# SiLU times gate: loads and stores moved to GpSimd's one queue, each transfer as a single packet

## The chip, the cores and the metric

The kernel runs on one core of one Trainium2 chip. A core has five engines with their own instruction streams: TensorE (not used here), VectorE (DVE in the profile), ScalarE (ACT), GpSimd (POOL) and SyncE (SP). Data moves between the chip's main memory (HBM) and the core's working memory (SBUF, 128 partitions) by 16 DMA engines. A transfer is issued from the queue of one of the engines; every issuer's transfers run on the same 16 DMA engines. The metric is device time in microseconds (us), the median of several runs.

## The reference

The input `x` is fp32 of shape 32 x 512 x 2048. The last dimension is cut in two halves, and the output, 32 x 512 x 1024, is SiLU of the first half times the second:

```
x1, x2 = x[..., :1024], x[..., 1024:]
silu_x1 = x1 * (1 / (1 + np.exp(-x1)))
out = silu_x1 * x2
```

That is 134.22 MB read and 67.11 MB written, with one SiLU and one multiplication per output element.

## The kernel before

The input is taken as 16,384 rows of 2048 numbers and cut into 16 tiles of 1,024 rows. In a tile each of the 128 partitions holds K = 8 rows that follow each other in HBM, so a partition's part of a load is one run of 65,536 B and its part of a store one run of 32,768 B. A load moves 8 MiB, a store 4 MiB.

There are two input buffers (`xt`) and two output buffers (`ot`), from two pools with `bufs=2`. Nothing is reordered by a scheduler (`manual_schedule`): each engine runs its instructions in the order of the program, and semaphores make an instruction wait for what it needs.

For tile i the kernel runs `silu` (line 86, ScalarE, from `xt` into `ot`), then `mul` (line 93, VectorE, in place in `ot`), then stores `ot` (line 112, issued on ScalarE's queue), then issues the load of tile i + 2 into the input buffer that has just come free (line 82, SyncE's queue). Loads 0 and 1 are issued ahead of the loop; load 0 is moved ahead of the program's first barrier by `issue_ahead_of_the_first_barrier`, which takes the first load that it finds, on whichever engine.

Two tiles are cut finer. Tile 0 is computed in four pieces of two rows per partition (KC_EDGE = 2), and its store is issued in five pieces, named in `OPENING` by partitions and rows: the first needs only the first piece of two rows. Tile 15 is computed in two halves (KS = 4), each stored by itself (line 120).

Loads and stores stand in two queues of their own, SyncE's and ScalarE's. A load has to wait until the multiplication of the tile that used its buffer is done, and a SiLU until the store that used its output buffer is done.

Of the kernel before, what the change touches and what calls it, by code (L numbers as in the profile page):

```python
# [1 line left out]

# [4 lines left out]


def issue_ahead_of_the_first_barrier(nc):

    head, body = nc.main_func.blocks[:2]
    load = next(ins for ins in body.instructions if type(ins).__name__ == "InstDMACopy")
    at = next(
        j for j, ins in enumerate(head.instructions)
        if ins.engine == load.engine and type(ins).__name__ == "InstDrain"
    )
    body.instructions = [ins for ins in body.instructions if ins.name != load.name]  # L20
    head.instructions = head.instructions[:at] + [load] + head.instructions[at:]


@with_exitstack
def kernel(
    ctx: ExitStack,
    tc: tile.TileContext,
    x: bass.AP,
    out: bass.AP,
):  # L30

    nc = tc.nc
    P = nc.NUM_PARTITIONS

    x_flat = x.flatten_outer_dims()  # L40
    out_flat = out.flatten_outer_dims()
    num_rows, in_cols = x_flat.shape
    half = in_cols // 2
    dt = x_flat.dtype

    K = 8
    KC_EDGE = 2
    KS = 4
    OPENING = [
        (slice(0, None, 4), slice(0, 2)),  # L50
        (slice(2, None, 4), slice(0, 4)),
        (slice(2, None, 4), slice(4, None)),
        (slice(0, None, 4), slice(2, None)),
        (slice(1, None, 2), slice(None)),
    ]
    PLAN = [K] * (num_rows // (P * K))

    in_pool = ctx.enter_context(tc.tile_pool(name="in_pool", bufs=2))
    out_pool = ctx.enter_context(tc.tile_pool(name="out_pool", bufs=2))

    plan = []
    row = 0
    for k in PLAN:
        plan.append((row, k))
        row += P * k
    assert row == num_rows
    n_tiles = len(plan)

    def view(flat, i):
        row0, k = plan[i]  # L70
        return flat[row0:row0 + P * k].rearrange("(p k) d -> p k d", k=k)

    nc.at_finalize(issue_ahead_of_the_first_barrier)


    ctx.enter_context(tc.manual_schedule())

    loaded = {}

    def load(i):  # L80
        xt = in_pool.tile([P, K, in_cols], dt, name="xt")
        nc.sync.dma_start(out=xt[:, :plan[i][1], :], in_=view(x_flat, i))
        loaded[i] = xt

    def silu(ot, xt, c, ce):
        nc.scalar.activation(  # L86
            out=ot[:, c:ce, :],
            in_=xt[:, c:ce, :half],
            func=mybir.ActivationFunctionType.Silu,
        )  # L90

    def mul(ot, xt, c, ce):
        nc.vector.tensor_mul(  # L93
            out=ot[:, c:ce, :],
            in0=ot[:, c:ce, :],
            in1=xt[:, c:ce, half:],
        )

    load(0)
    load(1)  # L100
    for i in range(n_tiles):
        xt = loaded.pop(i)
        ov = view(out_flat, i)
        ot = out_pool.tile([P, K, half], dt, name="ot")
        if i < n_tiles - 1:
            kc = KC_EDGE if i == 0 else K
            for c in range(0, K, kc):
                silu(ot, xt, c, c + kc)
                mul(ot, xt, c, c + kc)

            for ps, ks in OPENING if i == 0 else [(slice(None), slice(None))]:
                nc.scalar.dma_start(out=ov[ps, ks], in_=ot[ps, ks])
            if i + 2 < n_tiles:
                load(i + 2)
            continue
        for c in range(0, K, KS):
            silu(ot, xt, c, c + KS)
            mul(ot, xt, c, c + KS)
        for c in range(0, K, KS):
            nc.scalar.dma_start(out=ov[:, c:c + KS], in_=ot[:, c:c + KS])  # L120


# [1 line left out]
_INS = ['x']  # L124
_OUTS = [((32, 512, 1024), 'float32')]


# [23 lines left out]
```

## Time and profile before

| What | Value |
|---|---|
| Time, median of 3 runs | 470.35 us (470.28 to 472.34) |
| Span of the profiled execution | 468.4 us |
| DMA: loads (queue q1) | 134.22 MB, 2304 packets, 66.4% of the 16 engines' span |
| DMA: stores (queue q10) | 67.11 MB, 2576 packets, 33.2% |
| Mean rate over the span | 430 GB/s |
| VectorE busy | 139.3 us (30%), 14 full multiplications of 8.69 us |
| ScalarE busy | 114.1 us (24%), 14 full SiLUs of 7.03 us |
| GpSimd busy | 0.2 us |
| Load, median from issue to landing | 35.1 us |
| Full store, median from issue to landing | 42.2 us |

The profile is of one execution. Its span goes from the first to the last instruction on the core; a time on the device has some launch and end around it, and the median of the runs is 1.95 us above this span. The profiled execution's time from launch to end is not given apart from the span.

In the slices each digit is the busy share of one fortieth of the span, in tenths. In the DMA row it is the mean over the 16 engines. The share of a queue is the time that its packets took out of 16 engines times the span. The chain is the work that ended last, followed back from the last instruction; each of its lines has a start, a length and what ran. In the timeline a line has a start, a length, the engine (with a q for its queue), the line of the program, the instruction and how many of them, and in brackets the idle time ahead of it and what ended it. The trace also holds a record of each DMA packet: queue, start, length and size.

### The profile page before, as it was taken

What the parts mean: (1) busy time and instruction counts of PE and PEld (TensorE: products, weight loads), DVE (VectorE), ACT (ScalarE), POOL (GpSimd) and SP (SyncE); (2) the same over time, 40 slices, a digit from 0 to 9 for tenths busy, and PEclk for the clock granted to TensorE, in tenths of its full rate; (3) what the DMA queues carried; (4) which work ended last, traced back from release to release, by engine and by line L of the source; (5) the groups of instructions that cost most, each with busy time, mean ns of one, the idle gap of its engine ahead of it and who ended that gap; (6) DMA issues with size and microseconds to landing.
All of it is one profiled execution on the core that took longest, in us unless ns stands there. A gap on an engine that the chain in (4) does not pass through costs nothing.

```text
span 468.4 us, 185 instructions
## 1 busy us (share of the span) xinstructions
DVE 139.3 (30%) x20; ACT 114.1 (24%) x21; POOL 0.2 (0%) x4
## 2 busy tenths in 40 slices
DVE  0070600704207042070520605116061150602543
ACT  1142305005050050601406014060230602306060
POOL 0000000000000000000000000000000000000000
DMA  9899999999999999999999999899999899999998
GB/s 442 364 470 425 448 403 403 493 403 403 448 465 431 403 442 409 493 403 414 437 448 448 403 448 465 386 448 439 411 493 442 372 439 493 403 448 403 428 423 358
DMA packets 4880, 201.33 MB, mean 430 GB/s; under 512 B 592, under 2 KB 592, under 8 KB 592
## 3 DMA queue, kind: packets, MB, share of 16 engines
q1 hardware_dynamic: 2304, 134.22, 66.4%
q10 hardware_dynamic: 2576, 67.11, 33.2%
HBM read 134.22 MB, written 67.11 MB: 430 GB/s over the span
## 4 chain that ended last, share of the span: by engine, by line
DMA 72%; DVE 14%; ACT 11%; DVEq 1%; issue 0%
DMA out_dram<-ot 63%; DVE ot L93 14%; ACT ot L86 11%; DMA xt<-in_x_dram 9%; DVEq L146 1%
## 5 line engine op out<-in xcount | busy, mean ns | idle before, releaser
L93 DVE TENSOR_TENSOR ot<-ot,xt 128x8192 f32<-128x8192 f32 (+2 forms) x20 | 139.3, 6983 | 321.1 <-ACT ot L86 321.1
L86 ACT ACTIVATE ot<-xt 128x8192 f32<-128x8192 f32 (+2 forms) x20 | 112.8, 5661 | 340.2 <-DMA out_dram<-ot 305.8
L86 ACT ACT_TABLE_LOAD x1 | 1.3, 1283 | 0.8 <-PEq L135 0.8
L135 POOL MEMSET const-bfloat16-1.0<- 128x1 bf16 x1 | 0.1, 102 | 0.0
L135 POOL MEMSET const-uint8-127<- 128x1 uint8 x1 | 0.1, 102 | 0.0
L135 POOL MEMSET const-float32-1.0<- 128x1 f32 x1 | 0.1, 99 | 0.0
L135 POOL MEMSET const-float32-0.0<- 128x1 f32 x1 | 0.1, 98 | 0.2 <-issue 0.2
## 6 DMA issues: line engine op xcount, KB each, us to landing
out_dram<-ot ACTq DMA_DIRECT2D x14, 4096.0 KB, 42.2
out_dram<-ot ACTq DMA_DIRECT2D x3, 2048.0 KB, 6.9
out_dram<-ot ACTq DMA_DIRECT2D x2, 512.0 KB, 17.6
out_dram<-ot ACTq DMA_DIRECT2D x1, 768.0 KB, 28.2
xt<-in_x_dram SPq DMA_DIRECT2D x16, 35.1
out_dram<-ot ACTq DMA_DIRECT2D x1, 256.0 KB, 11.3
```

Source lines behind the costliest of these rows:

```text
L86: nc.scalar.activation(out=ot[:, c:ce, :], in_=xt[:, c:ce, :half], func=mybir.ActivationFunctionType.Silu,)
L93: nc.vector.tensor_mul(out=ot[:, c:ce, :], in0=ot[:, c:ce, :], in1=xt[:, c:ce, half:],)
L135: nc = _bacc.Bacc("TRN2", target_bir_lowering=False, num_devices=1)
L146: with _tile.TileContext(nc) as tc:
```

## The change

Loads 0 and 1 stay on SyncE's queue and the last tile's two stores on ScalarE's. All others, stores 0 to 14 and loads 2 to 15, are issued from GpSimd's queue, in the order store 0, load 2, store 1, load 3 and so on, each with `single_packet=True`: on each DMA engine, a transfer's descriptors make up one packet. Tile 0 is still computed in four pieces, but stored as one transfer, and `OPENING` is gone. Nothing else in the computation changes.

```
@@ tile_split_silu_mul_kernel @@
-    OPENING = [
-        (slice(0, None, 4), slice(0, 2)),
-        (slice(2, None, 4), slice(0, 4)),
-        (slice(2, None, 4), slice(4, None)),
-        (slice(0, None, 4), slice(2, None)),
-        (slice(1, None, 2), slice(None)),
-    ]
@@ load(i) @@
         xt = in_pool.tile([P, K, in_cols], dt, name="xt")
-        nc.sync.dma_start(out=xt[:, :plan[i][1], :], in_=view(x_flat, i))
+        if i < 2:
+            nc.sync.dma_start(out=xt, in_=view(x_flat, i))
+        else:
+            nc.gpsimd.dma_start(out=xt, in_=view(x_flat, i), single_packet=True)
         loaded[i] = xt
@@ the loop over tiles @@
-            for ps, ks in OPENING if i == 0 else [(slice(None), slice(None))]:
-                nc.scalar.dma_start(out=ov[ps, ks], in_=ot[ps, ks])
+            nc.gpsimd.dma_start(out=ov, in_=ot, single_packet=True)
             if i + 2 < n_tiles:
                 load(i + 2)
```

## The prediction

> **What bounds the kernel now.** I read the time slices first, then the DMA queues, the chain of waits, the groups by form, and last the trace's packet records.
>
> ```profile
> span 468.4 us, 185 instructions
> ...
> DVE  0070600704207042070520605116061150602543
> ACT  1142305005050050601406014060230602306060
> ...
> DMA  9899999999999999999999999899999899999998
> ...
> DMA packets 4880, 201.33 MB, mean 430 GB/s; under 512 B 592, under 2 KB 592, under 8 KB 592
> ...
> q1 hardware_dynamic: 2304, 134.22, 66.4%
> q10 hardware_dynamic: 2576, 67.11, 33.2%
> ```
>
> The DMA row is at 9 nearly everywhere while VectorE and ScalarE are mostly idle. The two queues together fill 66.4 + 33.2 = 99.6% of the 16 engines' span. So the kernel is bound by the DMA engines, and a change can win only what is in the missing 0.4% (1.9 us) and in overhead inside packets. It can lose whatever leaves the engines without work.
>
> The chain, in order of time, shows the opening and the steady period:
>
> ```profile
> 0.78 42.99 DMA xt<-in_x_dram
> ...
> 43.79 7.04 ACT ot L86
> ...
> 50.85 8.70 DVE ot L93
> ...
> 59.58 45.22 DMA out_dram<-ot
> ...
> 104.82 7.04 ACT ot L86
> ...
> 111.88 8.70 DVE ot L93
> ...
> 120.60 42.19 DMA out_dram<-ot
> ...
> 162.82 7.04 ACT ot L86
> ```
>
> Load 1 has landed by 43.77. In the steady part two tiles take 162.82 - 104.82 = 58.00 us, so one takes 29.00. Computing a tile takes 7.04 + 8.70 and three steps of 0.02, that is 15.8. The reader should see that 15.8 is far below 29.00: arithmetic matters only if the engines run out of queued transfers while it goes on.
>
> The packet records say what those 29.00 us are. A load is 8 packets of 65,536 B on each engine, 2.418 us each (19.34), and a full store 8 of 32,768 B, 1.213 us each (9.70); together 29.04. A packet of 16,384 B takes 0.611, so doubling it to 32,768 adds 0.602, and 2 x 0.602 leaves 0.009 us that every packet costs whatever its size. Each engine gives the two queues turns: one load packet, one store packet, and again. The 4 B completion packet takes a turn too: at 42.5 us the engines run a store packet of 16,384 B, and only behind it, at 43.05 to 43.5, load 1's completion.
>
> The opening, by the timeline:
>
> ```profile
> 21.75 5.51 ACT L86 ACTIVATE ot<-xt 128x2048 f32<-128x2048 f32 x3 [19.70 <-DMA xt<-in_x_dram]
> 23.70 8.90 DVE L93 TENSOR_TENSOR ot<-ot,xt 128x2048 f32<-128x2048 f32 x4 [23.70 <-ACT ot L86]
> 26.02 0.55 ACTq L112 DMA_DIRECT2D out_dram<-ot  x1
> ...
> 28.22 6.19 ACTq L112 DMA_DIRECT2D out_dram<-ot  x4
> ```
>
> Tile 0 is multiplied by 32.60, and its store goes out in five pieces from 26.02 on, in between load 1's packets.
>
> **The change part by part.**
>
> Issues. 19 store issues leave ScalarE's queue (0.34 to 0.63 us each) and 14 load issues leave SyncE's (about 0.33); 15 stores and 14 loads come to GpSimd's queue, which had none. ScalarE's loss of the issues in the opening saves nothing: VectorE multiplies without a gap from 23.70 to 32.60 and sets when tile 0 is done. Behind a waiting store on GpSimd's queue stands only the load that needs the same tile's buffer, so no other work is held.
>
> Latency of a GpSimd issue. The trace has none. The nearest rows: the first load was issued at 0.00 and its first packet ran at 1.0, on idle engines; the store issued at 59.58 had its first packet at 62.91 (3.3), that of 26.02 at 31.02 (5.0), both on busy ones. So I take 1.0 to 5.0, 2.0 where the engines are idle (between the two nearer rows, closer to the idle one), 3.3 where they are busy.
>
> Steady state. Every transfer now stands in one line: store i-1, load i+1, store i, load i+2. When load i lands, store i-1 and load i+1 are queued, 29.04 us of work. Store i follows after 15.8 + 1.0 to 5.0, at most 20.8, so it is in line with at least 8.2 us to spare: cost nothing. The cover is gone only when a GpSimd issue takes over 13.2 us. ScalarE's wait moves from the store to the load, still off the path.
>
> Fewer packets. 29 transfers of 8 data packets become one each: 29 x 7 x 0.009 = 1.8 us less on each engine if the 0.009 belongs to the packet, nothing if it belongs to the descriptor. I take 0.9.
>
> The opening, where load 1 on SyncE's queue meets GpSimd's packets. Load 1's packets start at 21.02 on the first engine and every 2.418 after: the seventh would start at 35.5, the eighth at 37.95, and end at 40.4. Store 0 is issued whole at 32.6; with 3.3 it is there at 35.9, so its turn is at 37.95, ahead of load 1's eighth packet (with 1.0 ahead of the seventh, with 5.0 still ahead of the eighth). Its turn is a packet of 8 descriptors: 9.70 instead of 1.21. Then load 1 has one turn of 2.42, then load 2's packet of 19.34, and what is left of load 1, its completion packet at the least, waits behind it. All four transfers are done when their bytes are: 21.4 (slowest engine) + 19.34 + 9.70 + 19.34 = 69.8. Load 1 lands 0.3 later (load 0's last completion packet was at 21.38, its landing at 21.7), at 70.1 instead of 43.8. Load 2 has landed too, and nothing is queued: store 1 and load 3 need tile 1's multiply. That ends at 70.1 + 15.8 = 85.9, the first packet comes at 87.9. The engines stand still from 69.8 to 87.9: 18.1 us, between 17.1 (latency 1.0) and 21.1 (5.0). After that tile 2 is computed under store 1 and load 3, and the line stays full.
>
> The end. When load 15 lands, store 14 is in line for 9.70. The first half of tile 15 is multiplied 3.61 + 4.42 = 8.0 later; its store on ScalarE's queue, 1.0 to 3.3 on, comes 0.7 early to 1.6 late. I take 0.
>
> **The sum**, from the span's start: 87.9, then 13 loads with 13 stores at 29.00 (377.0), two stores' worth more (19.4), less 0.9, and 1.3 from the last packet to the span's end (0.3 to land; landed 467.4, ended 468.4): 484.7. The same sum for the kernel before, without idle time, is 69.8 + 377.0 + 19.4 + 1.3 = 467.5, 0.9 under its span. The median of the runs, 470.35, is 1.95 over the profiled span, so I forecast 484.7 + 1.95 = 486.7 us.
>
> **Two rules against the rows.** The trace of before has no GpSimd transfer, so it cannot show what a multiply does to one; it has a 128x8192 multiply at 8.69 us, and 20.3 us of idle VectorE ahead of each in the steady part. The Trainium skill, SBUF — State Buffer, "SBUF: two separate sides", warns that descriptors of GpSimd's transfers cannot be written while VectorE runs a two-port fast mode; no run here shows whether this multiply is one. By it, store 1 in the opening, issued just as tile 2's multiply starts, would be held 8.7 longer, and the sum would be 495.4. The other way, DMA: Bandwidth & Descriptors, "Issuing engines are not separate DMA queues", holds that all issuers share the same engines and only issue time changes; by that alone the sum is the time before, 470.35.
>
> **The rivals.**
>
> Load 1 is not caught. If GpSimd's own completion of store 0 takes a turn of its own, the order after store 0 is load 1's eighth packet, that completion, load 1's completion, and only then load 2. Load 1 lands at 40.4 + 9.7 + 0.3 = 50.4, tile 1 is multiplied by 66.2, and at 3.3 its store is there at 69.5, before load 2 ends at 69.8. What decides is whether load 1's completion gets its turn before load 2's packet starts at 50.1. For it: hardware queues give completions their own turn. Against: "single packet" may hold the completion too. Also here if GpSimd's latency is over 5.4 (37.95 - 32.6), so that store 0 comes after load 1's last data packet. Span 467.5 less 0 to 1.8, to at most the 468.4 of now: 467.6 to 470.35, about 469. Chance 0.26, and a third of it is below 468.0.
>
> The single packet is not honoured: descriptors keep their turns, load 1 shares them as now and lands near 44. The time is then 469 to 470.5. Chance 0.11.
>
> The software ring is slower per byte. Nothing in the trace speaks for it; its nearest row is small packets: a load cut into 16,384 B packets would take 4 x 0.611 = 2.444 per 65,536 B, 1.1% more on 14 x 19.34 + 15 x 9.70 = 416 us, 4.5 us. Without the opening's hole that gives 474.9; twice that, 479. Chance 0.13, nearly all slower.
>
> **How the numbers follow.** The forecast has 0.50: catching load 1 needs a latency under 5.4 us, where the rows go to 5.0, and a packet that is really one. Its own range: down by 1.0 of latency and 0.9 of packets to 484.8, up by 3.0, 0.9 and the end's 1.6 to 492.2. The range of 8 in 10 reaches down through most of the uncaught case, 468 to 490; what lies under 468 (0.11) and above 490 (some 0.05) is left out. No change within 0.5%, 2.35 us, is about what runs of this kernel can tell: 468.0 to 472.7. Slower is 0.50 and 0.12 of the ring, 0.62; faster 0.09 of the uncaught case and 0.02 of the others, 0.11; the same, 0.27.
>
> **What would show it.** Right: one stretch of DMA at 0 for some 18 us from about 70, load 1 landing near 70, 9s everywhere else, periods of 28.9 to 29.0, ScalarE waiting for loads. Wrong in the opening: load 1 landing at 44 to 51 and no hole. Wrong in the steady part: periods over 29.2, or a hole in each of them between a load's landing and the next store, which would mean a GpSimd issue that takes more than 13 us.

## The result, and the profile after

The changed kernel takes 475.41 us (median of 4 runs, 474.42 to 476.37) against 470.33 us (470.28 to 472.34). The ratio is 1.0102, with a 95% interval of 1.0078 to 1.0125. It is slower by 1%, about 5.1 us; I had forecast 16 us, by a hole in the opening, and a range that began at 468. The time lies in that range, but the loss has neither the size nor the place that I gave it.

The page of the changed kernel's profile, the lines that answer to those shown of before:

```profile
span 472.6 us, 176 instructions
...
DMA  9989999999999999999999999999999999999977
...
DMA packets 4752, 201.33 MB, mean 426 GB/s; under 512 B 528, under 2 KB 528, under 8 KB 528
...
q0 software_dynamic: 4176, 180.36, 88.4%
q1 hardware_dynamic: 288, 16.78, 8.6%
q10 hardware_dynamic: 288, 4.19, 2.1%
```

There is no slice at 0: the engines never stand still for 18 us. The row has an 8 in the third slice, and 7 and 7 at the end, where before it had 9 and 8. The queue that GpSimd feeds (q0) has 4,176 packet records for 29 transfers: 29 x 16 x 9, so eight data records and a completion on each engine for every transfer. The flag has not made one record of them, so the one packet per engine that I named in the change does not show in the records.

The timeline of the opening and of the end (start, length, engine, line, instruction; in brackets the idle time ahead of it and what ended it):

```profile
33.01 0.67 POOL L107 DMA_DIRECT2D out_dram<-ot  x1 [32.57 <-DVE ot L89]
33.68 0.54 POOL L78 DMA_DIRECT2D xt<-in_x_dram  x1
44.79 7.03 ACT L82 ACTIVATE ot<-xt 128x8192 f32<-128x8192 f32 x1 [15.62 <-DMA xt<-in_x_dram]
...
71.58 7.03 ACT L82 ACTIVATE ot<-xt 128x8192 f32<-128x8192 f32 x1 [19.76 <-DMA xt<-in_x_dram]
...
451.63 7.12 ACT L82 ACTIVATE ot<-xt 128x4096 f32<-128x4096 f32 x2 [21.93 <-DMA xt<-in_x_dram]
455.28 8.76 DVE L89 TENSOR_TENSOR ot<-ot,xt 128x4096 f32<-128x4096 f32 x2 [16.85 <-ACT ot L82]
459.73 4.68 ACTq L115 DMA_DIRECT2D out_dram<-ot  x2
```

Load 1 landed before 44.79, not at 70. ScalarE now waits for loads, as foreseen. Tile 2 starts at 71.58 and tile 15 at 451.63: 13 tiles in 380.05 us, 29.23 each, where the kernel before took 29.00. The 0.23 is what the first reading has to explain; 13 of them are 3.0 us.

The packet records say how. The trace does not name a packet's engine, but each engine runs its packets back to back, so the records can be sorted into 16 rows, and the ends of a load's eighth packets show how far the engines are apart:

```
                       load 2 ends (first to last engine)   load 15 ends (first to last engine)
before                 66.54 to  66.98   (0.44 apart)        443.54 to 443.98   (0.44)
changed kernel         70.38 to  71.12   (0.74)              447.44 to 451.20   (3.76)
```

In the kernel before the 16 engines stay 0.44 us apart from load 1 to load 15. In the changed kernel the foremost engines keep a period of 29.0 (their loads begin at 51.0, 80.1, 109.1 and so on to 428.1), and five others fall behind by some 0.2 us per tile: the slowest is 0.74, 0.87, 1.19, 1.64, 1.87, 2.24 and at last 3.76 behind. A tile can be computed only when its slowest engine is done. Until load 15 that costs nothing, since the queue is long. At the end it does. Busy time by stretch; the columns are start and end, length, GpSimd's busy time and count, TensorE's clock, the DMA engines' mean share and GB/s. First the changed kernel:

```profile
34.00:40.00 6.00, 0.22 (x1) 1.00 0.77 262
...
447.00:457.00 10.00, 0.00 (x0) 1.00 0.95 410
457.00:461.00 4.00, 0.00 (x0) 1.00 0.41 172
461.00:472.60 11.60, 0.00 (x0) 1.00 0.80 339
```

and the kernel before:

```profile
443.00:453.00 10.00, 0.00 (x0) 1.00 0.97 419
453.00:457.00 4.00, 0.00 (x0) 1.00 0.98 422
457.00:468.40 11.40, 0.00 (x0) 1.00 0.84 358
```

Between 457 and 461 the DMA engines of the changed kernel are busy 41%: eleven engines have ended store 14 between 457.12 and 457.81 and wait for tile 15's first store, which could not be issued before 459.73; the other five end store 14 between 460.55 and 460.88. All the engines run tile 15's stores from 460.62 on; in the kernel before it was 456.97.

That makes the account of the 4.2 us between the two profiled spans. The foremost engine ends store 14 at 457.12 instead of 456.85, 0.27 later; the slowest at 460.88 instead of 457.29, 3.59 later, so 3.32 more comes from falling apart. The last stores end 3.97 later (470.99 instead of 467.02), 0.4 more, and 0.2 lies behind. For the 0.27, the stretch from 34 to 40 us shows a cause: when store 0 starts, every engine's running load packet takes 3.3 to 3.6 us instead of 2.42. With it the opening's load packets take 1.04 us per engine over 2.418 each; in the kernel before, with the five small pieces, they take 0.80. The difference is 0.24.

### The profile page after: what moved, and what is told of

Its sections match the earlier page's. It is cut to its first block, busy times and chain, and to the rows that moved or that the text cites. A ratio compares the mean times of both kernels' runs of the same rounds, so it can differ in the third digit from the quotient of the medians.

```text
span 472.6 us, 176 instructions
## 1 busy us (share of the span) xinstructions
DVE 139.4 (29%) x20; ACT 114.1 (24%) x21; POOL 15.8 (3%) x33
## 3 DMA queue, kind: packets, MB, share of 16 engines
q0 software_dynamic: 4176, 180.36, 88.4%
## 4 chain that ended last, share of the span: by engine, by line
issue 84%; DMA 9%; POOL 3%; DVE 1%; DVEq 1%; ACT 1%; POOLq 0%; ACTq 0%
DMA xt<-in_x_dram 9%; POOL out_dram L107 2%; POOL xt L78 1%; DVE ot L89 1%; DVEq L141 1%; ACT ot L82 1%; POOLq L78 0%; ACTq L82 0%; POOLq L130 0%
## 5 line engine op out<-in xcount | busy, mean ns | idle before, releaser
L107 POOL DMA_DIRECT2D out_dram<-ot x15 | 8.1, 541 | 423.2 <-DVE ot L89 423.2
L78 POOL DMA_DIRECT2D xt<-in_x_dram x14 | 7.6, 543 | 0.0
```

Of the source, the lines that this page charges most:

```text
L78: nc.gpsimd.dma_start(out=xt, in_=view(x_flat, i), single_packet=True)
L107: nc.gpsimd.dma_start(out=ov, in_=ot, single_packet=True)
```

## The experiments

**The changed kernel again, without its flag, on a hardware queue, and with software loads alone.** Four kernels ran on one chip. The first is the changed kernel as it is:

> The changed kernel again, beside the other three on one chip. Three theories for its 4.2 us over the span of before. Ring: on some engines a transfer whose descriptors GpSimd writes costs about 0.25 us more at the end of each load, so the slowest engine falls back 3.2 us by load 15. Flag: the single-packet flag does that. Line: loads and stores behind one another in one queue do it. All three expect 1.010 times before here, load 15 landing near 451 and some engines 3 us ahead of others by then.

The second leaves the flag out:

```
-            nc.gpsimd.dma_start(out=xt, in_=view(x_flat, i), single_packet=True)
+            nc.gpsimd.dma_start(out=xt, in_=view(x_flat, i))
...
-            nc.gpsimd.dma_start(out=ov, in_=ot, single_packet=True)
+            nc.gpsimd.dma_start(out=ov, in_=ot)
```

> The changed kernel without the single-packet flag, on loads and stores. Ring and Line: as with it, 1.010 of before, load 15 landing near 451, store 0 taking turns with load 1 as it does with the flag. Flag: about 1.002 (only the opening's loss of about 0.5 us is left), load 15 landing near 448.

The third keeps the order, store i then load i+2, and issues it on SyncE's queue:

```
-            nc.gpsimd.dma_start(out=xt, in_=view(x_flat, i), single_packet=True)
+            nc.sync.dma_start(out=xt, in_=view(x_flat, i))
...
-            nc.gpsimd.dma_start(out=ov, in_=ot, single_packet=True)
+            nc.sync.dma_start(out=ov, in_=ot)
```

> The same order, store i then load i+2 in one line, but issued on SyncE's hardware queue. Ring: the engines stay together (spread at the end of each load under 0.5 us), periods of 29.0, time 0.998 to 1.002 of before. Line: the engines drift apart as in the changed kernel, 1.008 to 1.010. Flag: as Ring.

The fourth is the kernel before with its loads from 2 on on GpSimd's queue:

```
-        nc.sync.dma_start(out=xt[:, :plan[i][1], :], in_=view(x_flat, i))
+        (nc.sync if i < 2 else nc.gpsimd).dma_start(out=xt, in_=view(x_flat, i))
```

> The kernel before, with loads 2 to 15 issued on GpSimd's queue without the flag; stores stay on ScalarE's queue in the opening's five pieces. Ring: some engines lose up to 0.25 us per load, time 1.004 to 1.010 of before, unless the store packet whose turn comes next hides it. Line and Flag: 0.998 to 1.002.

Measured against before: 1.0115 (1.0102 to 1.0129) for the changed kernel, 1.0120 (1.0105 to 1.0135) without the flag, 1.0102 (1.0088 to 1.0115) on the hardware queue, 1.0046 (1.0014 to 1.0078) with software loads alone. The flag makes no difference that these runs can tell. GpSimd's queue (`software_dynamic` in the profile, so I call what is issued there software loads and stores, and their descriptors software descriptors) adds 0.13% at the most likely, with intervals that overlap. The hardware queue alone, with neither GpSimd nor flag, loses as much. The page of that kernel:

```profile
span 473.6 us, 174 instructions
...
DMA  9989999999999999999999999999999999999968
...
q1 hardware_dynamic: 4464, 197.13, 96.8%
q10 hardware_dynamic: 288, 4.19, 2.1%
```

and its end by stretch:

```profile
447.00:457.00 10.00, 0.00 (x0) 1.00 0.97 416
457.00:461.50 4.50, 0.00 (x0) 1.00 0.25 109
461.50:473.60 12.10, 0.00 (x0) 1.00 0.82 347
```

Nothing in it is software (q1 is SyncE's queue), and it ends like the changed kernel, with the engines waiting at 457 to 461.5. Its spread grows from 0.82 at load 2 to 4.96 at load 15; the changed kernel again has 4.88 there, and 5.39 without the flag. So Ring and Flag fall as causes of the main loss, and Line stands: loads and stores behind one another in one queue. Line alone does not explain the fourth kernel, though, whose loads and stores have two queues and which still loses 0.5%. Its runs went from 470.27 to 478.32 us, and in the one that was profiled, 477.45, the engines are 6.4 us apart at load 15. One run does not explain the mean of the others, but two queues did not keep the engines together in it.

**What slows a packet.** For each load packet between 60 and 440 us I took its excess over 2.418 us, and how much of its time other engines spent on store packets (as a share of 16 engines):

```
share of other engines' stores      before              changed kernel      one hardware queue
                                   n   mean excess     n   mean excess     n   mean excess
none                                0                1198     0 ns       1167     0 ns
0.00 to 0.10                     1588     0 ns        250    10 ns        270     6 ns
0.10 to 0.40                       92     0 ns        185    32 ns        198    29 ns
over 0.40                           0                  42   228 ns         39   263 ns
```

In the single line no load packet is slowed that has the others' stores nowhere beside it. Those that run while more than 40% of the others' time goes on stores take some 0.23 to 0.26 us more. They are the last packets of a load on engines that are late. An engine that is late so meets more stores at the next load and gets later: I called this Step. In the kernel before, loads and stores take turns on every engine and the engines are in step, so a load packet never meets more than a fifth of the others' stores.

The table leaves a rival that fits as well, because the share of stores and a packet's place in its load go together here. Of the 18.07 us of excess in the changed kernel, summed over the engines, 17.99 are in the eighth and last packet of a load, and most of that on the five late engines, which lose 0.24 to 0.27 us per load. Among the first seven packets of a load, 160 ran beside stores with a share of 0.10 to 0.40, and none took longer. So what is slowed is a late engine's last packet before it turns to the store; that the others' stores do it is not shown by the table.

**Copies within SBUF in place of the stores.** This should tell writing to HBM from the turn in direction:

```
-    out_pool = ctx.enter_context(tc.tile_pool(name="out_pool", bufs=2))
+    out_pool = ctx.enter_context(tc.tile_pool(name="out_pool", bufs=1))
...
+    aside_pool = ctx.enter_context(tc.tile_pool(name="aside_pool", bufs=1))
+    aside = aside_pool.tile([P, K, half], dt, name="aside")
...
-            nc.sync.dma_start(out=ov, in_=ot)
+            nc.sync.dma_start(out=aside, in_=ot)
```

> The one hardware queue again, but stores 0 to 14 are left out: in their place each tile's result is copied aside within SBUF, the same bytes on the same engines at the same place in the line (one output buffer instead of two), so HBM is only read until the last tile. New theory, Step: a load packet is slowed (by 0.2 us and more) while other engines write to HBM, so engines that have fallen out of step fall further behind at the end of each load. Step expects load packets of 2.42 us throughout and a spread at the end of each load that stays under 1 us. If turning from a load to a transfer in the other direction costs time in the engine itself, the last packet of each load is still long and the spread grows to 3 us or more, as before.

It took 527.58 us in its one run. The copies' own packets are slowed, 32 us per engine of excess over 1.213 us each, so it does not decide what I built it for. Two things can be read. While the engines were in step (loads 2, 3 and 4: 0.68 apart each time) no load packet was slowed, though each load turned into a copy. After the copies had knocked the engines apart, load packets that had copies on other engines beside them for a fifth of the time or more took 0.3 us more on the mean as well. So it need not be HBM's writes that slow a load; where the two meet stays open.

**An engine put behind in the kernel before.**

```
...
     load(0)
     load(1)
+    lag_pool = ctx.enter_context(tc.tile_pool(name="lag_pool", bufs=1))
+    lag = lag_pool.tile([P, 3 * 1024], dt, name="lag")
+    nc.scalar.dma_start(out=lag[:4], in_=x_flat[:6].rearrange("r d -> (r d)").rearrange("(p f) -> p f", p=4))
```

> The kernel before, with one small extra load at the start, 12 KB on each of four partitions into a tile that nobody reads, so that a few engines start 0.45 us behind the others; two queues, turns as before. Step: once the engines are out of step by more than before's 0.44 us, load packets meet other engines' stores, some take 2.6 us and more, the spread grows to several us, time 1.003 to 1.015 of before. If only a single line of loads and stores drifts, the spread stays near 0.9 us and the time within 0.998 to 1.002.

Measured 1.0024 (1.0015 to 1.0034). The extra transfer put the engines further apart than I had reckoned, 1.39 us at load 0. From load 4 on 15 engines keep their places to within 0.1 us, the latest of them 1.50 behind the first; the 16th is 2.02 behind at load 4 and 5.24 at load 15, 0.29 more per load, as in the single line. So an engine can fall back in two queues too, where Line alone expects every spread to stay: a single line is not needed for it. The price was small, 0.24%, under the range that Step gave from 0.3% on. The profiled run took 474.10 us, the other ten 470.96 to 472.00, so the drift is shown for that one alone.

The same trace speaks against the others' stores as the cause. In it 115 load packets between 60 and 440 us ran beside stores with a share of over 0.40, and their mean excess is 2 ns. The 16th engine loses its 3.3 us in the second, third and fourth packets of its loads, none in the eighth, and from load 4 on the engine that is 1.50 behind loses nothing. So being late beside others' stores is not enough. Why just one engine falls back here and five in the changed kernel stays open; the trace does not name the engines, so it cannot say whether they are particular ones.

**Store 0 whole, the rest as before.**

```
-            for ps, ks in OPENING if i == 0 else [(slice(None), slice(None))]:
+            for ps, ks in [(slice(None), slice(None))]:
```

> The kernel before with one part of the change alone: tile 0's store issued whole after its last piece, on ScalarE's queue; loads and the other stores as before. Step: between 0.998 (engines keep in step) and 1.012 (the first store knocks them apart); the trace's spread tells which, and the two go together. If the single line is the cause: 0.998 to 1.003 whatever the spread.

Measured 1.0067 (1.0052 to 1.0082), and here my Step was wrong, and Line too: the engines stay 0.5 us apart to the end, no load packet is slowed after the opening, and still 2.9 us are lost. The end of this kernel by stretch:

```profile
447.00:457.00 10.00, 0.00 (x0) 1.00 0.85 367
457.00:459.60 2.60, 0.00 (x0) 1.00 0.00 0
459.60:470.80 11.20, 0.00 (x0) 1.00 0.88 375
```

From 457.0 to 459.6 all engines stand still. They have ended store 14 and wait for tile 15's first store. That wait is set by the order of bytes. With two queues that take turns, whatever is stored late in the opening stays late all the way: when load 15's last packet ends, 11.0 store packets per engine are left in the kernel before, and 6.9 here. Each is 1.21 us, so 13.3 us of cover against 8.3, and tile 15's first store comes 10.6 us after the last load packet (459.67 - 449.07). The five pieces of OPENING, which stand in the kernel's first 80 us, pay off in its last 15.

In the changed kernel the line itself leaves store 14 behind load 15: 8 packets, 9.70 us of cover, and tile 15's first store came 9.42 after the last load packet (460.62 - 451.20). For engines in step that is enough, as I had predicted. So this loss is not a part of the changed kernel's.

Beside the one hardware queue this kernel isolates the line: both store tile 0 whole and both use hardware queues alone. In two queues the engines are 0.5 us apart at load 15, in one line 4.96.

**Stores on GpSimd's queue, loads on SyncE's.**

```
-                nc.scalar.dma_start(out=ov[ps, ks], in_=ot[ps, ks])
+                (nc.scalar if i == 0 else nc.gpsimd).dma_start(out=ov[ps, ks], in_=ot[ps, ks])
```

> The kernel before with stores 1 to 14 on GpSimd's queue without the flag; loads on SyncE's, store 0 in five pieces on ScalarE's. Step: as with software loads, 1.000 to 1.010, in line with the spread. If software descriptors cost nothing by themselves and only a single line drifts: 0.998 to 1.002.

Measured 1.0023 (1.0006 to 1.0040), inside Step's range and at the edge of the other's. In the profiled execution, whose span of 469.0 is 0.6 over before's, the engines stay together, 0.71 apart at load 3 and 0.80 at load 15. Software descriptors in two queues can run at nearly the speed of before.

**Stops that bring the engines together.**

```
+    mark_pool = ctx.enter_context(tc.tile_pool(name="mark_pool", bufs=1))
+    mark = mark_pool.tile([P, 16], dt, name="mark")
...
+            if i in (5, 10):
+                nc.sync.dma_start(out=mark[:1, i:i + 1], in_=loaded[i + 1][:1, 0, :1])
             nc.sync.dma_start(out=ov, in_=ot)
```

> The one hardware queue, but at tiles 5 and 10 SyncE first waits until load 6 (load 11) has landed on all engines, by a 4-byte copy out of that tile, and only then issues store 5 (10) and the load behind it: all engines start again together. Step: the spread at the end of a load, 2.6 us and more at load 6, is back under 1 us at load 7 and load 12 and grows from there; by load 15 it is 1 to 2.5 us instead of 4.8. The two stops cost some 2 to 4 us each, so the time is 1.008 to 1.018 of before. If what a late engine loses per load does not depend on its being late, the slow engines lose 0.25 to 0.3 per load in every stretch, from the first load after a stop on.

The spread at the end of the loads, from the packet records:

```
load                      2     3     4     5     6     7     8     9     10    11    12    13    14    15
one hardware queue       0.82  0.99  1.40  2.03  2.60  3.14  3.14  3.94  3.89  4.05  4.58  4.58  4.58  4.96
with stops at 6 and 11   0.91  1.22  1.50  2.03  2.03  0.83  1.05  1.00  1.29  1.29  0.69  0.96  1.13  1.14
```

After a stop the engines are back within 1 us and end 1.14 apart instead of 4.96. From load 7 to 10 the spread grows by 0.46, from 12 to 15 by 0.45, 0.15 per load, half of the 0.25 to 0.3 that a fixed loss would make it. That speaks for a loss that depends on being late; but in this kernel's own opening, from 0.91 on, it grew by 0.37 per load up to load 5, so a start under 1 us does not set the pace alone. At loads 6 and 11, behind which no store stood in the queue, the spread did not grow at all (2.03 and 1.29, as at the loads before) and no load packet took longer. So in the single line the loss belongs to the passage from a load to a store. The price of a stop was misjudged: the time is 1.0287 (1.0268 to 1.0307) of before, where I expected up to 1.018. Load 15 ends 7.2 us later than without the stops, and after each the first load's eighth packets, those ahead of the next store, are slowed much as at the first store (1.36 and 1.19 us on the mean).

**Whether a flagged transfer is one turn.** Tile 0's store in four transfers of small runs, with and without the flag:

```
+            if i == 0:
+                for r in (0, 4):
+                    for c0 in (0, half // 2):
+                        nc.gpsimd.dma_start(out=ov[:, r:r + 4, c0:c0 + half // 2],
+                                            in_=ot[:, r:r + 4, c0:c0 + half // 2], single_packet=True)
...
```

> The changed kernel, with tile 0's store cut into four GpSimd transfers whose runs are 2,048 B (4 rows by 512 columns), each a single packet by its flag: 32 descriptors, 64 KiB, on each engine. The question is why store 0 in the changed kernel took turns with load 1 after every 32,768 B. If a turn is a packet and the flag makes one, all 32 runs of a transfer stand between two of load 1's packets. If turns go by bytes or descriptors whatever the flag, load 1's packets come after one or a few of the runs, as without the flag.

> The same four small transfers without the flag. If the flag makes a turn of a transfer: only one or a few runs of 2,048 B stand between two of load 1's packets here, against 32 with it. If it changes nothing: as with it.

The DMA queues with the flag:

```profile
DMA packets 5696, 201.33 MB, mean 423 GB/s; under 512 B 576, under 2 KB 576, under 8 KB 1600
...
q0 software_dynamic: 5120, 180.36, 88.2%
```

and without it:

```profile
DMA packets 5696, 201.33 MB, mean 424 GB/s; under 512 B 576, under 2 KB 576, under 8 KB 1600
...
q0 software_dynamic: 5120, 180.36, 88.4%
```

The records are the same: two runs of 2,048 B stand in one of 4,096 B (0.16 us), 16 for each of the four transfers on an engine, 1,024 in all. The turns are the same too. One engine of each, from the packet records (start, size, how many in a row):

```
with     30.93 65,536 x1 | 33.46 4,096 x1 | 33.62 65,536 x1 | 36.10 4,096 x1 | 36.26 65,536 ...
without  31.08 65,536 x1 | 33.52 4,096 x1 | 33.67 65,536 x1 | 36.16 4,096 x1 | 36.31 65,536 ...
```

Between two of load 1's packets stands one record of 4,096 B on each of the 16 engines, with the flag as without it. For transfers of this kind a turn is a record, and I saw no effect of the flag. Whether it is dropped on the way or has nothing to do with turns, these runs do not tell.

## Why the prediction was wrong, point by point

**"Its turn is a packet of 8 descriptors: 9.70 instead of 1.21."** This step failed, and with it the forecast. Store 0's turn was one record of 32,768 B. One engine of the changed kernel runs: store record at 39.03, load 1's eighth packet at 40.24, store record at 42.65, load 1's completion at 43.86. Load 1 landed at 44.8, the idle 18.1 us were 0. I had put the chance that a single packet is not honoured at 0.11 and gave it a landing near 44, which is what came, and 469 to 470.5 us, which is not. The Trainium skill, DMA: Bandwidth & Descriptors, "Queues, rings and completion order", has an engine drain a whole packet, typically 9 to 17 descriptors, before it goes to the next queue; in the turns of the changed kernel and of the two kernels with small transfers the engine changed queues after one record, of 32,768, 65,536 or 4,096 B.

**"Steady state ... cost nothing."** The cover in the queue was as reckoned, and GpSimd's issues are short: 0.53 us, none of them late. What failed is the period of 29.00 taken over from before. It rests on 16 engines in step, which the single line does not keep. The measured period is 29.23, 3.0 us over 13 tiles, and 3.3 of the 4.2 us between the spans are engines out of step. No term of the sum stood for this.

**"Fewer packets ... I take 0.9."** The changed kernel has eight data records per transfer and engine, of 2.418 and 1.213 us as before: 0 saved.

**Latency of a GpSimd issue, 1.0 to 5.0.** The issue of store 0 at 33.01 was first seen on the engines at 38.92, 5.9 us later; on SyncE's queue, issued at 32.71, the first store record came at 41.36, but there behind all of load 1. A record can start only when the load packet ahead of it ends, and load 1's seventh packets, begun at 35.52 to 35.99 with no store there yet, were slowed and ended from 38.92 on. So the latency lies between about 3.0 and 5.9 us: my 3.3 for busy engines is not contradicted, but the lower bound of 1.0 is out for them.

**"The end ... I take 0."** The step was right for engines in step, and wrong for these: the eleven foremost stand still for 2.8 to 3.6 us (457.81 to 460.62, and 457.12 to 460.74).

**The two rules.** In the changed kernel no multiply ran while GpSimd issued a transfer (tile 2's ended at 87.33, the issue was at 87.63). In the kernel with flagged small transfers two issues did fall among tile 0's multiplies, from 28.62 on for 1.66 us; the two behind the last multiply took 1.50, so the issues themselves were not held up. Their first record came at 33.24, behind a load packet and 0.5 us after the last multiply had ended (32.72), so whether descriptors were held until then these runs do not decide. That all issuers share the same engines holds as far as the issuer goes: GpSimd's and SyncE's line differ by 0.1 to 0.2%. But with store 0 whole in both, one hardware line takes 475.43 us and two hardware queues 473.25, and they lose it in different places; that is more than issue time.

**A reading.** The prediction puts load 1's completions in the kernel before at 43.05 to 43.5; the records have 42.96 to 43.40. Nothing in the sum rests on it.

**The third rival, "slower per byte".** Its 474.9 is close to the measured 475.4 for a wrong reason: the same loss appears on a hardware queue.

## What to carry to other kernels

Where a kernel is bound by its transfers, look at the 16 engines one by one and not at their mean: a tile waits for the slowest, and a few engines out of step can cost a per cent while the DMA row shows 9s. One line of long loads and long stores let five of the 16 fall behind, on either kind of queue; two hardware queues that take turns kept them together in the kernel before and with store 0 whole, though not once an engine had been put far behind. And the order of bytes in the opening decides what is left to hide the last tile's arithmetic: count the store packets that stand behind the last load.

## What was not expected of the hardware

- Load packets of 65,536 B took 2.418 us to within 18 ns when no other engine was storing (0 ns of mean excess over 1,198 of them in the changed kernel). In the changed kernel the last packet of a load took 0.24 to 0.27 us more on the mean on five of the 16 engines. Stores on other engines are not enough for it: 115 load packets of the kernel with the lag ran with over 40% of the others' time on stores, and took 2 ns more. What does it stays open.
- The first transfer out of SBUF slows the packet that each engine is running by about 1 us (1.0 in the changed kernel, 1.2 on one hardware queue, 1.2 with a copy within SBUF, 0.8 in the kernel before, spread over its small pieces), and so does the first passage from a load to a store after a stop (1.36 and 1.19).
- The single-packet flag changed neither records nor turns nor time (1.0115 with it, 1.0120 without).
